# Gathering 48 of an encoder layer's tokens on all 128 partitions: 32 tokens in quarters and 16 in eighths, in place of 48 in halves on 96

## The chip, the cores and the metric

One core of a Trainium2 chip runs the whole layer. The metric is the device time of one execution in microseconds; the slowest (here the only) core counts.

## The reference, cut to what matters

One encoder layer on x of 512 tokens by 2048: a linear attention and a dilated window attention, then a mixer of 16,384 single-neuron experts. Only the mixer matters for the change:

```python
qry = (xt @ w_query).reshape(T, 8, 2, 128)
sc = jnp.einsum('thcd,hckd->thck', qry, sub_keys)          # 128 keys on either side, 8 heads
top_s, top_i = lax.top_k(sc, 16)                           # then the best 16 of the 256 pairs a head
idx   = expert numbers, 8 * 16 = 128 a token;  gates = softmax of their scores
u   = expert_down[idx]                                     # (tokens, 128, 2048)
act = gelu(einsum('tkd,td->tk', u, xn))
out = einsum('tk,tkd->td', gates * act, expert_up[idx])    # x = x + out
```

Every token has 128 slots, each with an expert's number and a gate. Both expert tables are 16,384 rows of 2048 float32, 8192 B a row.

## The kernel before

The layer goes through stages: the projections with both attentions (up to about 700 us of the profiled execution), the output projection, the queries with scores and top-k (about 900 to 1150 us), a stage that makes gate matrices (1200 to 1460 us), and the expert loop (1499 us to the end).

The 512 tokens are divided. **336 dense tokens** pass through all 16,384 experts on PE: `downT` (128 blocks `e` of 128 experts) gives the pre-activations, Gelu and the gates follow, and `upT` adds up the output. Each float32 product is made of three (`mm3`, lines 126 to 128), from a high part that ACT casts (line 77) and a low part that DVE subtracts (line 85; in the early blocks POOL does some). **128 tokens and 48 tokens** are gathered: for every slot an indirect DMA brings a row of an expert table per token, and DVE does the rest.

- The 128 tokens (`xn`, `idx[0]`, `gate[0]`, `ga[0]`) stand on 128 partitions, and a gather event handles one slot of each: 128 events a table.
- The 48 tokens (`xb`, `idx[1]`, ...) stand twice, on partitions 0 to 47 and 48 to 95. Lane h of a token handles half of its slots, so an event moves 96 rows and there are 64 of them. The two halves of the output are added on PE with the matrix `qs` at the end (line 1048).

`events` (line 1014) lists them: down rows of the 48, down rows of the 128, up rows of the 48 and one event that adds the tokens' x, up rows of the 128 and one such event; 386 in all. `gather(n)` (line 1036) fetches two events ahead, on POOL's queue, into one of three buffers `row`; for a down row DVE multiplies and sums (line 1042, into a column of `ga`), for an up row it adds the weighted row (line 1057). So an issue on POOL waits until DVE has read the buffer that it writes. `gather_next` is called 21 times in the gate stage, four times in the two blocks behind it, and then by `after()` (line 1273): spread evenly over the 448 steps of the loop but the last ten. A step is 24 matmuls: half of a `downT` block (`act_half`) or a granule of `upT`. After the last down event two steps go by before `weights_of_slots` makes the weights of the up rows.

The loop has 16 super-blocks of eight `e`. The first four have no `downT` steps: their 32 blocks were computed earlier and wait in DRAM (`pre_d`). Weights, `pre_d` and gates come on SP's queue.

**The gate stage.** For the dense tokens the gates become a matrix of 128 by 128 keys a token: one-hot rows `e` (DVE, line 1184, two buffers), times the gate (line 1187) and copied (ACT, line 1189), a matmul a token (line 1206), and a copy into `gs` (ACT, line 1208), which holds GT = 48 tokens. A full `gs` goes to DRAM `gt_d` on ACT's queue (line 1210). In the loop `fetch_gates` (line 1230) brings them back for four `e` at a time: 128 partitions, DENSE/GT groups, and in each a contiguous piece of 4 * GT numbers. The first two fetches are issued by POOL, in its queue between gathers.

The 48 tokens are prepared in three places: `turned_x` (line 776) transposes them with the others in the query stage, `gathered_slots` (line 1098) makes `idx` and `gate` and moves them to both halves by one matmul with the matrix `used` (line 1108), and POOL makes `used` and `qs` (lines 1009 and 1166).

Of the kernel before, what the change touches and what calls it, by code (L numbers as in the profile page):

```python
# [10 lines left out]
F32 = mybir.dt.float32  # L11
# [15 lines left out]
LB = 64  # L27
SPARE = 16
NB2 = LB - SPARE
PARTS = 128 // LB  # L30
GT = 48
LANES = (128, PARTS * NB2)
# [5 lines left out]
SLOTS = 128  # L38
LOW = -3.4e38
# [66 lines left out]
def layer(ctx, tc, A, out_t, out_g, out_b):  # L106
# [567 lines left out]
    rg = gn.tile([128, 2], F32, name="rg")  # L674
# [60 lines left out]
    xb = xnp.tile([LANES[1], D], F32, name="xb")  # L735
# [6 lines left out]
    sel_b = sp.tile([128, 3, SLOTS // PARTS], F32, name="sel_b")  # L742
# [19 lines left out]
    with ExitStack() as st:  # L762
# [13 lines left out]
        def turned_x(k, b):  # L776

            bank = pa()
            if b:
                t = tq.tile([128, 4, PARTS, NB2], F32, name="xr4")  # L780
                nc.scalar.copy(t, xq[:, 4 * k:4 * k + 4, SPARE:LB].unsqueeze(2).to_broadcast([128, 4, PARTS, NB2]))
            for c in range(4):
                src = t[:, c].rearrange("p a b -> p (a b)") if b else xq[:, 4 * k + c, LB:]
                nc.tensor.transpose(bank[:LANES[b], c * 128:(c + 1) * 128], src, ident)
            cs, n = slice(512 * k, 512 * k + 512), NB2 if b else 128
            xr = tq.tile([128, 512], F32, name="xr", bufs=2)
            nc.scalar.copy(xr[:n, :], bank[:n, :])
            nc.vector.tensor_tensor((xb if b else xn)[:, cs], bank[:LANES[b]], gains[k][:LANES[b]], op=OP.mult)
            nc.scalar.dma_start((x1b_d if b else x1g_d)[:, cs], xr[:n, :])
            if b and k + 2 < 4:  # L790
                gain_rows(k + 2)
# [4 lines left out]
        def rstd2():  # L796
            b = pa()
            for t in range(NB):
                nc.tensor.matmul(b[:, t:t + 1], sq[:, t * 128:(t + 1) * 128], ones[:, 0:1], start=True, stop=True)
            for h in range(PARTS):  # L800
                nc.tensor.matmul(b[LB * h:LB * h + LB, 4:5], sq[:, BASE:BASE + LB], ones[:, 0:1], start=True, stop=True)
            r = rsqrt(b[:, :5], 5, 1.0 / D)
            nc.vector.tensor_copy(rg, r[:, 3:5])
            return r
# [169 lines left out]
        for h in range(8):  # L974
            o = [pj() if h else pa() for _ in range(2)]
            for q in range(4):
# [19 lines left out]
                if 1 <= h < 5 and q % 2 == 0:  # L996
                    turned_x(h - 1, q // 2)
# [4 lines left out]
        n_slots = (SLOTS, SLOTS // PARTS)  # L1002
        idx = [slot.tile([128, n], I32, name=f"idx{b}") for b, n in enumerate(n_slots)]
        gate = [slot.tile([128, n], F32, name=f"gate{b}") for b, n in enumerate(n_slots)]
        ga = [slot.tile([128, n], F32, name=f"ga{b}") for b, n in enumerate(n_slots)]
        qs = slot.tile([128, NB2], F32, name="qs")
        lane = slot.tile([128, 2 * n_slots[1] + 1], F32, name="lane")
        used = slot.tile([128, PARTS, NB2], F32, name="used")
        nc.gpsimd.tensor_copy(used, ident.rearrange("p (a b) -> p a b", b=LB)[:, :, SPARE:])
        used = used.rearrange("p a b -> p (a b)")  # L1010
# [3 lines left out]
        events = [(up, b, k) for up in range(2) for b in (1, 0) for k in range(n_slots[b] + up)]  # L1014
        TURN = sum(n_slots)

        def fetch_rows(n):

            if n < len(events):
                up, b, k = events[n]  # L1020
                fetched[n] = t = rows.tile([128, D], F32, name="row", bufs=3)
                m = LANES[b]
                if k == n_slots[b]:
                    nc.gpsimd.dma_start(t[:NB2 if b else 128, :], (x1g_d, x1b_d)[b])
                else:
                    nc.gpsimd.indirect_dma_start(out=t[:m], out_offset=None, in_=A["up" if up else "down"],  # L1026
                                                 in_offset=bass.IndirectOffsetOnAxis(ap=idx[b][:m, k:k + 1], axis=0))

        def weights_of_slots():

            for b in range(2):
                g = ga[b][:LANES[b]]
                nc.scalar.activation(g, g, AF.Gelu_apprx_tanh, scale=rg[:LANES[b], b:b + 1])
                nc.vector.tensor_tensor(g, g, gate[b][:LANES[b]], op=OP.mult)

        def gather(n):
            fetch_rows(n + 2)
            up, b, k = events[n]
            m = LANES[b]
            t, x, g = fetched.pop(n)[:m], (xn, xb)[b][:m], ga[b][:m]  # L1040
            if not up:
                nc.vector.tensor_tensor_reduce(t, t, x, 1.0, 0.0, OP.mult, OP.add, g[:, k:k + 1])  # L1042
            elif k == n_slots[b]:
                if b:
                    for c in range(4):
                        cs = slice(c * 512, c * 512 + 512)
                        bank = pa()
                        nc.tensor.matmul(bank[:NB2, :], qs[:m], x[:, cs], start=True, stop=True)
                        nc.vector.tensor_tensor(t[:NB2, cs], t[:NB2, cs], bank[:NB2, :], op=OP.add)
                    nc.gpsimd.dma_start(out_b, t[:NB2, :])  # L1050
# [47 lines left out]
        def gathered_slots():  # L1098
# [4 lines left out]
            n, m = n_slots[1], LANES[1]  # L1103
# [3 lines left out]
            b = pa()  # L1107
            nc.tensor.matmul(b[:m, :2 * n + 1], used, lane, start=True, stop=True)
            nc.vector.tensor_copy(idx[1][:m], b[:m, 0:n])
            nc.scalar.copy(gate[1][:m], b[:m, n:2 * n])  # L1110
            nc.scalar.copy(rg[:m, 1:2], b[:m, 2 * n:2 * n + 1])
# [51 lines left out]
    with ExitStack() as st:  # L1163
        gp = pool(st, "gp")
        io4 = gp.tile([128, 128, 4], BF16, name="io4")
        nc.gpsimd.tensor_tensor(qs, ident[:, 0:NB2], ident[:, NB2:2 * NB2], op=OP.add)
# [11 lines left out]
        def one_hots(n):  # L1178
# [4 lines left out]
            e = gp.tile([128, 2, 128, 4], BF16, name="e", bufs=2)  # L1183
# [238 lines left out]
```

## Time and profile before

| | us |
|---|---|
| median of the three runs (lowest, highest) | 3423.83 (3418.21, 3429.88) |
| the profiled execution's own time | 3438.33 |
| its span, first to last instruction | 3436.6 |
| PE busy | 3196.3 (93%) |
| DVE busy | 2496.3 (73%) |
| ACT busy | 1163.0 (34%) |
| POOL busy | 1057.9 (31%) |
| DMA queue q1 (SP's loads), share of 16 engines' span | 33.3% |
| DMA queue q0 (POOL's gathers), share of 16 engines' span | 32.3% |
| moved by all queues | 811.09 MB |

The busy times are of engines that work side by side; they don't add up to the span. A share over the whole span mixes stages with different limits, so the stages are read apart. PE's matmuls are pipelined, and their records overlap.

### The profile page before, as it was taken

To read this page: it belongs to the slowest core of one execution; us is meant where nothing else is said; L and a number is where in the kernel's file an instruction comes from. 1 tells how busy PE (TensorE), PEld (TensorE's weight loads), DVE (VectorE), ACT (ScalarE), POOL (GpSimd) and SP (SyncE) were. 2 spreads that over 40 slices of the span, in tenths; PEclk is the share of its full clock that TensorE was granted. 3 is DMA by queue.
4 is the path that set the end of the run, shared out by engine and by line. 5 is a ranking of instruction groups with operands and counts; after the bars stand their busy time and mean duration, and the time that the engine had idled before them with its cause. 6 is when DMAs were issued, how large, how long until landed. Compare 5 with 4: busy or idle time off the path is not lost.

```text
span 3436.6 us, 47809 instructions
## 1 busy us (share of the span) xinstructions
PE 3196.3 (93%) x19012; PEld 2947.0 (86%) x19012; DVE 2496.3 (73%) x3830; ACT 1163.0 (34%) x1879; POOL 1057.9 (31%) x788
## 2 busy tenths in 40 slices
PE   8999999999999899967779999999889899999999
PEld 6777878788999899867679999899788799999999
DVE  5545353554468889957779888888777788989887
ACT  4334443443222355522223232232222222323322
POOL 3111010101245765512233333333332233333331
PEclk9999999999999999989899999999999999999999
DMA  4232222233322467699989999999899989999987
GB/s 144 86 97 78 86 74 86 86 131 139 101 94 78 133 225 256 227 283 259 249 280 352 352 354 358 358 363 339 242 266 271 266 315 350 365 347 382 354 344 269
DMA packets 151088, 811.09 MB, mean 236 GB/s; under 512 B 14736, under 2 KB 55024, under 8 KB 60912
## 3 DMA queue, kind: packets, MB, share of 16 engines
q1 hardware_dynamic: 86688, 390.69, 33.3%
q0 software_dynamic: 53888, 382.48, 32.3%
q10 hardware_dynamic: 10288, 34.87, 2.8%
q8 instruction: 149, 2.44, 0.3%
q14 instruction: 75, 0.61, 0.1%
HBM read 768.92 MB, written 39.06 MB: 235 GB/s over the span
## 4 chain that ended last, share of the span: by engine, by line
PE 39%; issue 24%; DVE 16%; DMA 10%; POOL 9%; ACT 2%; POOLq 0%; DVEq 0%; ACTq 0%
PE pj L128 10%; PE pj L126 10%; PE pj L127 10%; POOL row L1026 8%; DMA row<-in_up_dram,idx 5%; DMA wr4x<-in_upT_dram 3%; DVE e L1184 3%; DVE xn L1057 2%; DMA wr16x<-in_downT_dram 2%; DVE w L1187 2%; DVE row L1042 2%; DVE wl2x L85 1%; PE pa L609 1%; PE pa L550 1%; DVE wl8x L85 1%
## 5 line engine op out<-in xcount | busy, mean ns | idle before, releaser
L85 DVE TENSOR_TENSOR wl2x<-wr4x,wh2x 128x1024 fp32r<-128x1024 f32 x382 | 468.8, 1231 | 399.7 <-ACT wh2x L77 399.1
L128 PE MATMUL pj<-ah,wl2x 128*128 128x336 f32 x2048 | 673.7, 329 | 63.6 <-DVE wl2x L85 63.0
L126 PE MATMUL pj<-ah,wh2x 128*128 128x336 f32 x2048 | 665.1, 325 | 69.3 <-ACT wh2x L77 69.1
L127 PE MATMUL pj<-al,wh2x 128*128 128x336 f32 x2048 | 660.4, 322 | 2.4 <-DVE al L1259 2.4
L128 PE MATMUL pa<-yh,wl8x 128*128 128x336 f32 x1920 | 623.0, 324 | 40.9 <-DVE wl8x L85 38.8
L77 ACT CAST wh2x<-wr4x 128x1024 fp32r<-128x1024 f32 x382 | 394.6, 1047 | 750.6 <-DMA wr4x<-in_upT_dram 452.3
L126 PE MATMUL pa<-yh,wh8x 128*128 128x336 f32 x1920 | 622.3, 324 | 19.6 <-ACT wh8x L77 19.6
L127 PE MATMUL pa<-yl,wh8x 128*128 128x336 f32 x1920 | 613.4, 319 | 0.0
L1026 POOL DMA_INDIRECT row<-in_up_dram,idx x192 | 320.3, 1668 | 665.3 <-DVE xn L1057 381.9
L1026 POOL DMA_INDIRECT row<-in_down_dram,idx x192 | 308.4, 1606 | 629.0 <-DVE ga L1042 620.3
L128 PEld LDWEIGHTS pj<-ah,wl2x 128*128 128x128 f32 x2048 | 396.5, 194 | 92.8 <-DVE wl2x L85 90.9
L126 PEld LDWEIGHTS pj<-ah,wh2x 128*128 128x128 f32 x2048 | 397.9, 194 | 78.9 <-ACT wh2x L77 77.6
L128 PEld LDWEIGHTS pa<-yh,wl8x 128*128 128x128 f32 x1920 | 365.1, 190 | 63.3 <-DVE wl8x L85 56.1
L127 PEld LDWEIGHTS pj<-al,wh2x 128*128 128x128 f32 x2048 | 397.5, 194 | 4.4 <-DVE al L1259 3.3
L126 PEld LDWEIGHTS pa<-yh,wh8x 128*128 128x128 f32 x1920 | 366.9, 191 | 22.6 <-ACT wh8x L77 22.6
L127 PEld LDWEIGHTS pa<-yl,wh8x 128*128 128x128 f32 x1920 | 366.7, 191 | 0.0
L77 ACT CAST wh8x<-wr16x 128x1024 fp32r<-128x1024 f32 x256 | 265.3, 1046 | 248.0 <-DMA wr16x<-in_downT_dram 184.1
L85 DVE TENSOR_TENSOR wl8x<-wr16x,wh8x 128x1024 fp32r<-128x1024 f32 x200 | 249.1, 1246 | 99.9 <-ACT wh8x L77 99.7
L1042 DVE CUSTOM_DVE_ANT_0 row<-row,xn 128x2048 f32<-128x2048 f32 x128 | 292.5, 2285 | 26.7 <-DMA row<-in_down_dram,idx 26.7
L1057 DVE SCALAR_TENSOR_TENSOR xn<-row,ga,xn 128x2048 f32<-128x2048 f32 x127 | 297.9, 2346 | 10.2 <-DMA row<-in_up_dram,idx 10.2
L126 PE MATMUL pj<-wh2x,xh 128*128 128x512 f32 x704 | 284.8, 405 | 0.0
L127 PE MATMUL pj<-wl2x,xh 128*128 128x512 f32 x704 | 275.4, 391 | 1.3 <-DVE wl2x L85 1.3
(331 smaller groups left out, 5119.1 us busy)
## 6 DMA issues: line engine op xcount, KB each, us to landing
wr16x<-in_downT_dram SPq DMA_DIRECT2D x128, 1024.0 KB, 8.6
wr4x<-in_upT_dram SPq DMA_DIRECT2D x128, 1024.0 KB, 9.1
wr4x<-in_win_dram SPq DMA_DIRECT2D x47, 1024.0 KB, 4.9
gt_d<-gs ACTq DMA_DIRECT2D x7, 3072.0 KB, 12.4
g<-gt_d SPq DMA_DIRECT2D x30, 672.0 KB, 9.3
wr4x<-in_wout_dram SPq DMA_DIRECT2D x16, 1024.0 KB, 4.9
wr8x<-in_wq_dram SPq DMA_DIRECT2D x16, 1024.0 KB, 5.1
pre_d<-spill ACTq DMA_DIRECT2D x32, 168.0 KB, 4.4
```

What stands on the lines that cost most here:

```text
L77: self.nc.scalar.copy(hi, t)
L85: self.lo_engine[n].tensor_tensor(lo, t, hi.bitcast(F32), op=OP.subtract)
L126: nc.tensor.matmul(out, sh, mh, start=first, stop=False)
L127: nc.tensor.matmul(out, sh, ml, start=False, stop=False)
L128: nc.tensor.matmul(out, sl, mh, start=False, stop=last)
L550: nc.tensor.matmul(sc[u], qt[:, h, t * 128:(t + 1) * 128], kt[:, h, :], start=True, stop=True)
L609: nc.tensor.matmul(oo, vv[:, kb, h * 128:(h + 1) * 128], pt[u][:, kb, :], start=kb == 0, stop=kb == NB - 1)
L1026: nc.gpsimd.indirect_dma_start(out=t[:m], out_offset=None, in_=A["up" if up else "down"], in_offset=bass.IndirectOffsetOnAxis(ap=idx[b][:m ...
L1042: nc.vector.tensor_tensor_reduce(t, t, x, 1.0, 0.0, OP.mult, OP.add, g[:, k:k + 1])
L1057: nc.vector.scalar_tensor_tensor(x, t, g[:, k:k + 1], x, op0=OP.mult, op1=OP.add)
L1184: nc.vector.tensor_tensor(e, ij[:, :, ts].unsqueeze(2).to_broadcast([128, 2, 128, 4]), io4.unsqueeze(1).to_broadcast([128, 2, 128, 4]), op ...
L1187: nc.vector.tensor_tensor(w[:, 0], e[:, 0].rearrange("p k t -> p t k"), gd[:, ts].unsqueeze(2).to_broadcast([128, 4, 128]), op=OP.mult)
```

## The change

The 48 tokens are divided again, into 32 and 16. The 32 stand four times on the 128 partitions, each copy with a quarter of the slots (32 events a table); the 16 stand eight times, with an eighth each (16 events). With the 128 tokens that makes 176 events a table, all on 128 partitions; the rows that are moved stay the same. Each group has its own `x` (`xc` is new), `idx`, `gate`, `ga`, `qs`, and its own last event. To make room, GT becomes 28: twelve stores of a smaller `gs` for seven, and in `fetch_gates` twelve pieces of 448 B a partition for seven of 768 B. `e` gets a third buffer. The core of the diff:

```diff
-PARTS = 128 // LB
-GT = 48
-LANES = (128, PARTS * NB2)
+TOK = (NA, 32, 16)
+COL = (LB, SPARE, SPARE + 32)
+GT = 28
+N_SLOTS = tuple(SLOTS * n // 128 for n in TOK)
...
         def turned_x(k, b):
-            bank = pa()
+            bank, n, first = pa(), TOK[b], COL[b]
             if b:
-                t = tq.tile([128, 4, PARTS, NB2], F32, name="xr4")
-                nc.scalar.copy(t, xq[:, 4 * k:4 * k + 4, SPARE:LB].unsqueeze(2).to_broadcast([128, 4, PARTS, NB2]))
+                m = 128 // n
+                t = tq.tile([128, 4, 128], F32, name="xr4")
+                nc.scalar.copy(t.rearrange("p c (a b) -> p c a b", b=n), xq[:, 4 * k:4 * k + 4, first:first + n].unsqueeze(2).to_broadcast([128, 4, m, n]))
...
-                if 1 <= h < 5 and q % 2 == 0:
-                    turned_x(h - 1, q // 2)
+                if 1 <= h < 5 and q < 3:
+                    turned_x(h - 1, q)
...
+        for b in (1, 2):
+            n = TOK[b]
+            qs[b] = slot.tile([128, n], F32, name=f"qs{b}")
+            for a in range(128 // n):
+                if a == 0:
+                    nc.gpsimd.tensor_copy(qs[b], ident[:, 0:n])
+                else:
+                    nc.gpsimd.tensor_tensor(qs[b], qs[b], ident[:, n * a:n * a + n], op=OP.add)
+            used[b] = sp.tile([128, 2, n], F32, name=f"used{b}")
+            nc.gpsimd.tensor_copy(used[b], ident.rearrange("p (a b) -> p a b", b=LB)[:, :, COL[b]:COL[b] + n])
...
-        events = [(up, b, k) for up in range(2) for b in (1, 0) for k in range(n_slots[b] + up)]
-        TURN = sum(n_slots)
+        events = [(up, b, k) for up in range(2) for b in (2, 1, 0) for k in range(N_SLOTS[b] + up)]
+        TURN = sum(N_SLOTS)
...
-                    nc.gpsimd.indirect_dma_start(out=t[:m], out_offset=None, in_=A["up" if up else "down"],
-                                                 in_offset=bass.IndirectOffsetOnAxis(ap=idx[b][:m, k:k + 1], axis=0))
+                    nc.gpsimd.indirect_dma_start(out=t, out_offset=None, in_=A["up" if up else "down"],
+                                                 in_offset=bass.IndirectOffsetOnAxis(ap=idx[b][:, k:k + 1], axis=0))
...
-            b = pa()
-            nc.tensor.matmul(b[:m, :2 * n + 1], used, lane, start=True, stop=True)
+            bank = pa()
+            for b in (1, 2):
+                k, m, c = N_SLOTS[b], 2 * TOK[b], 128 * (b - 1)
+                u = used[b].rearrange("p a b -> p (a b)")
+                for a in range(n // k):
+                    to = slice(m * a, m * a + m)
+                    for q, src in enumerate((lane[:, k * a:k * a + k], lane[:, n + k * a:n + k * a + k])):
+                        nc.tensor.matmul(bank[to, c + k * q:c + k * q + k], u, src, start=True, stop=True)
+                    nc.tensor.matmul(bank[to, c + 2 * k:c + 2 * k + 1], u, lane[:, 2 * n:], start=True, stop=True)
...
-            e = gp.tile([128, 2, 128, 4], BF16, name="e", bufs=2)
+            e = gp.tile([128, 2, 128, 4], BF16, name="e", bufs=3)
```

How the list moves the gathers is seen on POOL, from the last gather of the gate stage on to the up rows of the 128 tokens (a number behind x counts rows that follow each other). Before:

```order
L1026 DMA row<-in_down_dram,idx_9887 96x2048
L1232 DMA g<-gt_d 128x7x192 x2
L1026 DMA row<-in_down_dram,idx_9887 96x2048 x41
L1026 DMA row<-in_down_dram,idx_9886 128x2048 x128
L1026 DMA row<-in_up_dram,idx_9887 96x2048 x64
L1024 DMA row<-x1b_d 48x2048
L1026 DMA row<-in_up_dram,idx_9886 128x2048 x2
L1050 DMA out_dram<-row 48x2048
L1026 DMA row<-in_up_dram,idx_9886 128x2048 x126
```

And now, where idx_9933 is that of the 16 tokens and idx_9932 that of the 32:

```order
L1034 DMA row<-in_down_dram,idx_9932 128x2048
L1245 DMA g<-gt_d 128x12x112 x2
L1034 DMA row<-in_down_dram,idx_9932 128x2048 x25
L1034 DMA row<-in_down_dram,idx_9931 128x2048 x128
L1034 DMA row<-in_up_dram,idx_9933 128x2048 x16
L1032 DMA row<-x1b_d 16x2048
L1034 DMA row<-in_up_dram,idx_9932 128x2048 x2
L1057 DMA out_dram<-row 16x2048
L1034 DMA row<-in_up_dram,idx_9932 128x2048 x30
L1032 DMA row<-x1b_d 32x2048
L1034 DMA row<-in_up_dram,idx_9931 128x2048 x2
```

Behind the two gate fetches 41 gathers of 96 rows became 25 of 128, and of the 64 up gathers on 96 partitions 48 on 128 were left; a second event of x and a second output stand between them.

On POOL at the end of the query stage, where `used` is made ahead of the first weight differences `wl8x` that PE waits for, before:

```order
L886 TENSOR_TENSOR sel_d<-oh 128x2x2x16
L1009 COPY used<-ident 128x96
L85 TENSOR_TENSOR wl8x_9954<-wr16x_9706,wh8x_9952 128x1024
L85 TENSOR_TENSOR wl8x_10009<-wr16x_9706,wh8x_10007 128x1024
L834 CAST tf<-ti 128x64
```

And now:

```order
L889 TENSOR_TENSOR sel_d<-oh 128x2x2x16
L1015 COPY qs_9941<-ident 128x32
L1017 TENSOR_TENSOR qs_9941<-qs_9941,ident 128x32 x3
L1019 COPY used_9946<-ident 128x64
L1015 COPY qs_9948<-ident 128x16
L1017 TENSOR_TENSOR qs_9948<-qs_9948,ident 128x16 x7
L1019 COPY used_9957<-ident 128x32
L86 TENSOR_TENSOR wl8x_10017<-wr16x_9751,wh8x_10015 128x1024
L86 TENSOR_TENSOR wl8x_10072<-wr16x_9751,wh8x_10070 128x1024
L837 CAST tf<-ti 128x64
```

One small copy became fourteen small operations; the sum `qs` of line 1166, which stood later, is among them.

## Rows read from the trace of the kernel before

**Rows 1.** The page of the profile: busy time of each engine with its share of the span, and three lines of the 40 equal slices of the span (85.9 us each): PE's and the DMA engines' busy tenths, and GB/s moved.

```profile
PE 3196.3 (93%) x19012; PEld 2947.0 (86%) x19012; DVE 2496.3 (73%) x3830; ACT 1163.0 (34%) x1879; POOL 1057.9 (31%) x788
...
PE   8999999999999899967779999999889899999999
...
DMA  4232222233322467699989999999899989999987
...
GB/s 144 86 97 78 86 74 86 86 131 139 101 94 78 133 225 256 227 283 259 249 280 352 352 354 358 358 363 339 242 266 271 266 315 350 365 347 382 354 344 269
```

**Rows 2.** Busy time by stage. Columns: the stage (us from the span's start), its length, then busy us and number of instructions of PE, PEld, DVE, ACT and POOL, the granted TensorE clock as a share, the mean busy share of the 16 DMA engines, and GB/s.

```profile
900.00:1030.00 130.00, 129.55 (x977) 126.68 (x976) 76.07 (x353) 37.40 (x77) 51.11 (x40) 1.00 0.28 92
1100.00:1200.00 100.00, 89.25 (x573) 86.35 (x573) 81.95 (x352) 32.69 (x79) 71.80 (x55) 0.93 0.38 123
1200.00:1460.00 260.00, 243.38 (x1711) 238.06 (x1710) 238.94 (x224) 132.34 (x206) 149.35 (x64) 0.99 0.71 234
1460.00:1499.20 39.20, 21.46 (x122) 20.48 (x120) 14.35 (x16) 8.04 (x11) 6.42 (x6) 0.76 1.01 323
1499.20:1766.00 266.80, 208.64 (x1176) 194.89 (x1176) 190.50 (x236) 72.67 (x108) 64.32 (x39) 0.89 0.92 257
1836.20:2389.00 552.80, 525.53 (x3306) 510.98 (x3305) 483.65 (x535) 169.87 (x208) 181.11 (x113) 0.99 0.94 358
2413.00:2752.00 339.00, 293.63 (x1735) 279.81 (x1734) 262.03 (x226) 89.97 (x110) 101.84 (x61) 0.94 0.97 262
2793.00:3372.00 579.00, 551.68 (x3457) 534.89 (x3456) 514.73 (x447) 179.06 (x221) 196.86 (x119) 0.99 0.93 356
3372.00:3433.00 61.00, 59.52 (x384) 58.43 (x382) 40.67 (x43) 16.58 (x18) 5.79 (x5) 1.00 0.69 250
```

**Rows 3.** DMA queues in the stage 2413 to 2752 us (up rows of the 48 tokens): packets, MB, share of 16 engines' time. q0 carries what GpSimd issues (the gathers), q1 what SP issues (weights, gates).

```profile
q0 software_dynamic: 6759, 47.52, 56.2%
q1 hardware_dynamic: 9741, 41.18, 40.0%
```

**Rows 4.** The same for 2793 to 3372 us (up rows of the 128 tokens).

```profile
q0 software_dynamic: 17080, 124.33, 53.8%
q1 hardware_dynamic: 17664, 81.01, 38.5%
```

**Rows 5.** The same for 1499 to 1766 us (down rows of the 48 tokens).

```profile
q0 software_dynamic: 4558, 32.10, 46.8%
q1 hardware_dynamic: 13757, 36.25, 44.9%
```

**Rows 6.** Who waited for whom from 1836 to 3372 us: us in total, times, longest.

```profile
ACT wh2x L77 <- DMA wr4x<-in_upT_dram: 315.3, 64, 13.3
...
ACT wh8x L77 <- DMA wr16x<-in_downT_dram: 175.2, 46, 10.5
...
POOL row L1026 <- DVE ga L1042: 376.7, 115, 7.5
```

**Rows 7.** Groups of instructions by line and form, of the whole span: count, then busy us, mean ns of one, and the idle time ahead of them with what ended it.

```profile
L1042 DVE CUSTOM_DVE_ANT_0 row<-row,xn 128x2048 f32<-128x2048 f32 x128 | 292.5, 2285 | 26.7 <-DMA row<-in_down_dram,idx 26.7
...
L1057 DVE SCALAR_TENSOR_TENSOR xn<-row,ga,xn 128x2048 f32<-128x2048 f32 x127 | 297.9, 2346 | 10.2 <-DMA row<-in_up_dram,idx 10.2
...
L1026 POOL DMA_INDIRECT row<-in_down_dram,idx x192 | 308.4, 1606 | 629.0 <-DVE ga L1042 620.3 <-DVE al L1259 3.6 <-issue 3.1
```

**Rows 8.** DMA queue q10 (what ACT issues) from 206 to 246 us, where it stores the linear attention's turned output in pieces of 512 B: packets, MB, share of 16 engines' time.

```profile
q10 hardware_dynamic: 2109, 1.05, 8.9%
```

**Rows 9.** Instructions in order of time at the end of the one-hot stage (ACT's, then POOL's, then DVE's): start, us, engine, line, operation, and in brackets the idle time ahead of it and what ended it.

```profile
1464.77 0.33 ACTq L1210 DMA_DIRECT2D gt_d<-gs  x1
...
1479.88 1.04 ACT L77 CAST wh8x<-wr16x 128x1024 fp32r<-128x1024 f32 x1 [13.61 <-DMA pre<-pre_d]
...
1477.82 1.98 POOL L1232 DMA_DIRECT2D g<-gt_d  x2 [18.80 <-issue]
...
1494.64 2.29 DVE L1042 CUSTOM_DVE_ANT_0 row<-row,xb 96x2048 f32<-96x2048 f32 x1 [12.46 <-DMA row<-in_down_dram,idx]
```

**Rows 10.** The stores of the gates (L1210): time from issue to landing, least, median and most, of the seven.

```profile
DMA to landing us min/median/max: 10.4/12.4/13.7
```

**Rows 11.** The one-hot tiles' groups, by line and form (columns as in rows 7).

```profile
L1184 DVE TENSOR_TENSOR e<-ij,io 128x1024 bf16<-128x1024 bf16 x84 | 125.5, 1494 | 3.4 <-ACT ij L117 3.4
...
L1189 ACT CAST w<-e 128x512 f32<-128x512 bf16 x84 | 56.1, 669 | 115.1 <-DVE e L1184 113.9 <-DVE w L1187 1.2
```

**Rows 12.** Groups by line and form from 900 to 1200 us (columns as in rows 7): the transposes of the gathered tokens, the index matmul, and two set-up operations of POOL.

```profile
L784 PE MATMUL pa<-ident,xr 128*96 128x128 f32 x16 | 2.4, 272 | 0.0
...
L1108 PE MATMUL pa<-lane,used 128*96 128x129 f32 x2 | 0.4, 290 | 0.0
...
L1009 POOL COPY used<-ident 128x96 f32<-128x96 f32 x1 | 0.3, 263 | 0.0
...
L1166 POOL TENSOR_TENSOR qs<-ident 128x48 f32<-128x48 f32 x1 | 0.7, 733 | 0.0
```

**Rows 13.** The reduction of the 48 tokens at the end of the up rows, lines 1048 and 1049: count, ns of one (least, median, most), first and last start, and form.

```profile
L1048 PE MATMUL pa<-xb,qs x8: 592/592/630, 2766.3 to 2769.4; 96*48 96x512 f32 x8
L1049 DVE TENSOR_TENSOR row<-row,pa x4: 678/678/678, 2767.4 to 2770.0; 48x512 f32<-48x512 f32 x4
```

More of the change, by code (lines that the diff above doesn't have):

```diff
@@ L734, in layer @@
     xn = xnp.tile([128, D], F32, name="xn")
-    xb = xnp.tile([LANES[1], D], F32, name="xb")
+    xb = xnp.tile([128, D], F32, name="xb")
+    xc = xnp.tile([128, D], F32, name="xc")
     slot2 = work.enter_context(ExitStack())
@@ L799, in rstd2 @@
                 nc.tensor.matmul(b[:, t:t + 1], sq[:, t * 128:(t + 1) * 128], ones[:, 0:1], start=True, stop=True)
-            for h in range(PARTS):
+            for h in range(2):
                 nc.tensor.matmul(b[LB * h:LB * h + LB, 4:5], sq[:, BASE:BASE + LB], ones[:, 0:1], start=True, stop=True)
             r = rsqrt(b[:, :5], 5, 1.0 / D)
-            nc.vector.tensor_copy(rg, r[:, 3:5])
+            nc.vector.tensor_copy(rg[:, 0:2], r[:, 3:5])
             return r
@@ L1001, in layer @@
         slot = pool(ctx, "slot", side="right")
[L1002 to L1010, printed above, removed]
+        idx = [slot.tile([128, n], I32, name=f"idx{b}") for b, n in enumerate(N_SLOTS)]
+        gate = [slot.tile([128, n], F32, name=f"gate{b}") for b, n in enumerate(N_SLOTS)]
+        ga = [slot.tile([128, n], F32, name=f"ga{b}") for b, n in enumerate(N_SLOTS)]
+        lane = sp.tile([128, SLOTS + 1], F32, name="lane")
+        qs, used = {}, {}
+        for b in (1, 2):
[8 more added lines that the diff above has]
+            nc.gpsimd.tensor_copy(used[b], ident.rearrange("p (a b) -> p a b", b=LB)[:, :, COL[b]:COL[b] + n])
         spill = pool(ctx, "spill", side="right")
@@ L1021, in fetch_rows @@
                 fetched[n] = t = rows.tile([128, D], F32, name="row", bufs=3)
[L1022 to L1027 removed]
+                if k == N_SLOTS[b]:
+                    nc.gpsimd.dma_start(t[:TOK[b], :], (x1g_d, x1b_d[0:32], x1b_d[32:48])[b])
+                else:
+                    nc.gpsimd.indirect_dma_start(out=t, out_offset=None, in_=A["up" if up else "down"],
+                                                 in_offset=bass.IndirectOffsetOnAxis(ap=idx[b][:, k:k + 1], axis=0))
         def weights_of_slots():
[L1031 to L1034, printed above, removed]
+            for b in range(3):
+                g = ga[b]
+                nc.scalar.activation(g, g, AF.Gelu_apprx_tanh, scale=rg[:, b:b + 1])
+                nc.vector.tensor_tensor(g, g, gate[b], op=OP.mult)
         def gather(n):
```

36 lines of the change are left out of this document (17 added, 19 removed).

## The prediction

> **What bounds the kernel now.** I read the 40 slices first, then stages cut out of them, then the DMA queues of those stages. PE is busy 93% of the span, but not evenly: there are dips at 1400 to 1800 us and at 2400 to 2800 us, and in both the DMA engines are at 9 tenths while they move only some 250 GB/s; where PE is at 9, they move about 355 [rows 1]. The dips lie in the expert loop, which begins at 1499 us. I count it in steps: one pass of the weights' half or granule, 24 matmuls on PE (eight tiles by three products, or four tiles by two experts by three). So 1176 matmuls in 266.8 us are 49 steps of 5.45 us, 1735 in 339 us are 72.3 steps of 4.69, and the two stages between and behind take 3306/24 = 137.8 steps of 4.01 and 144 steps of 4.02. The last 16 steps, ten of which have no gather, take 3.81 [rows 2]. The two slow stages are those in which the 48 tokens are gathered on 96 partitions (first the down rows, then the up rows); in the others 128 tokens are gathered on 128.
>
> The DMA share does not tell them apart (0.92 and 0.97 against 0.94 and 0.93, same rows); the price of a row does. In the slow up stage the gathers' queue moved 47.52 MB, 5801 rows of 8192 B, in 56.2% of 16 engines' 339 us: 525 ns a row [rows 3]. In the quick up stage it is 53.8% of 16 x 579 us for 15,177 rows: 328 ns [rows 4]. In the slow down stage 1999 us for 3918 rows: 510 ns [rows 5]. The weights' queue suffers with it, 52.7 against 44.0 us per MB [rows 3, 4]. What ends last there is the DMA: the casts on ACT wait 315 and 175 us for weight transfers, while the gathers' issues wait for DVE, that is for a free buffer, and not the reverse [rows 6]. So DMA engines bound the slow stages; the quick stages lie close to three limits at once (DMA 0.93, PE 551.68 of 579, DVE 514.73).
>
> **The change, part by part.** I sum against the profiled execution's 3438.3 us; the median of the runs shown is 14.5 us below that.
>
> *Gathers.* Each pass has 176 events instead of 192 for the same 22,528 rows, and all are on 128 partitions. I take 328 ns a row for all: only the partition count differs between the two up stages. The ends are 328 (as quick) and 525 (no change). [...]
>
> Per step: before, 361 events (386 less 25 ahead of the loop) over 438 steps are 0.824, 79 rows a step with the 48 tokens and 105.5 with the 128; now 330 over 438 are 0.753, 96.4 rows everywhere.
>
> - First 49 steps. Need now 0.92 x 5.45 = 5.0 us of DMA a step. After: gathers 96.4 x 328/16 = 1.98 instead of 2.55; the other queue 2.45 [rows 2, 5] x 44.0/52.7 = 2.04; 0.11 of the rest and small pieces; together 4.13, at the same share 4.49 a step. Gain 47 us (58 at a share of 0.97). The next 15 steps gain 3.
> - The 282 quick steps need 0.93 x 4.02 = 3.74 a step; nine rows fewer take 0.19 off, small pieces add 0.04: 3.59. The last 16 steps need 0.69 x 3.81 = 2.63 and take 3.81. A straight line between the two gives 3.99 at 3.59; the lower end is 3.81. I take the middle, 3.90, since waits should grow quicker than the load. Gain 32 us (7 to 58).
> - The 72.3 slow up steps become such steps: 4.69 to 3.90, gain 57 us (51 to 64).
>
> DVE loses 32 products of some 2.3 us and POOL 32 issues of 1.6 [rows 7]. I count nothing for either: DVE's are covered by PE and DMA, and POOL waits for DVE [rows 6]. If DVE were the limit, its share is the rival below.
>
> *Small pieces of the gates.* GT = 28 instead of 48 makes a fetch of 672 KB 1536 pieces of 448 B instead of 896 of 768 B. No row has 448 B. Pieces of 512 B took 8.9% of 16 x 40 us over 2048, 28 ns at most [rows 8]; one of 768 B is then between 28 and 42. A fetch costs 0.3 to 1.1 us of DMA time more; I take 0.6, about 19 us over 32 fetches, which stands in the needs above. The other end is a doubled piece, 56 ns.
>
> *Stores of the gates, third buffer of e.* Twelve stores of 1.8 MB replace seven of 3.1. The last one stands on the path into the loop: issued at 1464.77, landed when POOL's gate fetch goes at 1477.8 after 18.8 us idle, and ACT's next store and cast wait as long [rows 9, 10]. 28/48 of 12.4 us saves 5 (0 to 8: the two fetches behind it, which hold up DVE's row for 12.5 us, get longer). The third buffer saves nothing: DVE waits 3.4 us in all before e, and ACT's 114 us before its half are for DVE, which is 92% busy there [rows 2, 11].
>
> *Ahead of the gathers.* 16 more transposes at 0.15 us and their copies stand where PE is full (129.55 of 130): 2.4 us on the path; DVE and ACT are at 76 and 37 of 130 there and cover theirs. 18 small matmuls of two records replace one, 34 records more at 0.15 to 0.29: 5 to 10 us of PE at a place that is 89% busy, between waits; I count 4. POOL gets 14 small operations for one ahead of the weight differences that PE waits for (and one fewer later): 13 at 0.26 to 0.73 is 3.4 to 9.5; half of that is hidden in POOL's 28% idle: 3. Together 9 (3 to 15) [rows 2, 12].
>
> *Last event of each group.* There are two reductions instead of one: four matmuls of two records and four DVE additions, about 3.4 us in a full loop; 4 [rows 13].
>
> Sum: -47 -3 -32 -57 +9 -5 +4 = -131 us, so 3307 for the profiled execution, 3293 at the median's level. The lower ends together give -175, **3249**; the upper ones -90, 3334.
>
> **Rivals.**
> 1. *Full relief*: the quick steps fall to 3.81, PE's own pace, as in the tail. -175: 3249. For it: PE is then the only full engine. Against: DVE stays near 0.86, in order, and the tail had hardly a gather.
> 2. *DVE or the chain of casts holds 4.01 a step.* For it: DVE is at 0.89 in the quick stages. Then the quick steps gain nothing, the slow up steps 49: -88, 3336.
> 3. *Short pieces cost double.* 1536 x 56 against what was taken is 2.8 us more a fetch: 0.175 a step lifts the need to 3.76, so the steps stay at 4.02 (the up stage of the 48 gains 48, the other 282 steps 0), and the first 64 steps, with a fetch every eight, lose 0.38 each, 24 of their 50. -66: 3358. For it: no row shows a fetch below 512 B. Against: 512, and the straight proportion to larger ones, show no step. [...]
> 4. *The price does not come from the partitions but from the 48 tokens' rows* (slower). The rows stay at 515 ns, now 128 at a time: a step of these stages needs 3.10 + 1.88 + 0.07 (the other queue as it is [rows 3]), 5.2 us at the same share, for 64 steps instead of 78, while 170 others take 3.92 instead of 155 at 4.02: 10 us more a pass. With the 8 us of the fixed parts that is +28: 3452. It decides from the price: 12,288 rows make 7.7 us per 10 ns, so above some 480 ns there is no gain left. Against: the down and the up tables both show it, with the same tokens' indices but other data, and the weights' transfers in the same stages slow too, though they read nothing of those rows.
>
> **How the numbers follow.** The forecast (3293, own range 3260 to 3325) gets 0.60, rival 1 0.15, rival 2 0.10, rival 3 0.10, rival 4 0.05. Forecast, 1, 2 and 3 are faster by more than 0.3% (10 us, about what a measurement here can tell); I move 0.02 of them to no change for a mixture of 2 and 3. Low is 3240, below rival 1; high is 3360, just above rival 3, which leaves out rival 4 and some tails.
>
> **What would show it.** Right: the price of a row on the gathers' queue is near 328 ns from the first stage of the loop to the last, at some 350 GB/s; there is no dip of PE at 2400 to 2800; the steps of the up pass take 3.9 us. Rival 1 shows as 3.8, rival 2 as 4.0 with DVE above 0.9 and DMA below 0.9, rival 3 as 4.0 with the weights' queue share grown by more than 3 points at the same MB, rival 4 as a price of 500 in the first third of each pass. The front is right if the loop begins at 1499 + 4 us (-5 to +15). The prediction is wrong if the slow stages' rows get cheaper and the steps there still take over 4.4 us.

## The result, and the profile after

The changed kernel takes **3280.7 us** (median of four runs, 3272.0 to 3285.0) against 3424.8 for the kernel before beside it: a ratio of 0.958, 95% interval 0.955 to 0.960. That is 12 us below the forecast and inside its own range, with two errors behind it that happen to cancel in part.

The profiled execution took 3272.0 us, the lowest of its four; that of before lay 14.5 us above its median. So the profiles differ by 166 us and the medians by 144, and the terms below, which come from profiles, add up to 166.

From the page after: the engines, PE, DMA and GB/s in 40 equal slices (81.8 us each), and the stores of the gates (KB each, median us to landing).

```profile
PE 3145.6 (96%) x19070; PEld 2922.8 (89%) x19070; DVE 2435.3 (74%) x3792; ACT 1168.0 (36%) x1890; POOL 1006.7 (31%) x770
...
PE   8999999999999989987899999999999999999999
...
DMA  4222222224322247779889999999989999999996
GB/s 152 78 88 96 75 94 71 91 97 146 125 90 79 80 145 264 265 270 340 322 335 339 358 362 358 360 350 352 348 334 364 349 343 358 358 364 358 358 358 251
...
gt_d<-gs ACTq DMA_DIRECT2D x12, 1792.0 KB, 6.7
```

Against [rows 1] the second dip of PE is gone and the first is shallower (8, 7, 8 in the 18th to 20th slice): from the 21st slice on PE stands at 9, and from the 19th on GB/s is never below 320 until the tail. By stage (columns as in [rows 2]):

```profile
900.00:1030.00 130.00, 121.27 (x895) 117.39 (x894) 68.29 (x305) 36.16 (x71) 43.44 (x33) 0.99 0.26 86
1473.20:1508.70 35.50, 25.07 (x157) 24.23 (x155) 18.94 (x19) 10.90 (x16) 10.59 (x8) 0.93 0.90 327
1508.70:1799.20 290.50, 259.49 (x1537) 247.51 (x1538) 237.15 (x288) 91.06 (x126) 78.47 (x48) 0.94 0.89 335
1799.20:2352.00 552.80, 543.00 (x3479) 533.29 (x3479) 487.65 (x542) 180.32 (x225) 177.88 (x109) 1.00 0.93 355
2410.00:2590.00 180.00, 179.94 (x1140) 174.00 (x1138) 159.95 (x150) 58.71 (x74) 57.62 (x37) 1.00 0.93 351
2660.00:3206.00 546.00, 538.18 (x3457) 530.50 (x3457) 489.36 (x433) 178.72 (x220) 187.47 (x108) 1.00 0.94 358
```

At 24 matmuls a step: 1537 are 64 steps of 4.54 us; 3479 are 145 steps of 3.81; 1140 (nearly all up rows of the 32 tokens) 47.5 steps of 3.79; 3457 are 144 steps of 3.79. The up stage that took 4.69 a step now goes at the pace of the others. The one row that got worse is the first: PE, which was full in 900 to 1030 us [rows 2], issues 82 matmuls fewer there.

The queues of three stages: 1508.7 to 1742 us (down rows of the 48 until 1649, then of the 128), 2410 to 2590 and 2660 to 3206 (columns as in [rows 3]).

```profile
q1 hardware_dynamic: 18440, 37.44, 46.8%
q0 software_dynamic: 5378, 39.09, 40.8%
...
q0 software_dynamic: 4954, 35.87, 50.8%
q1 hardware_dynamic: 8101, 27.14, 41.6%
...
q0 software_dynamic: 15636, 113.81, 52.3%
q1 hardware_dynamic: 22768, 80.97, 41.7%
```

The price of a row, share x 16 x stage / (MB / 8192 B): 319, 334 and 329 ns, where it was 510, 525 and 328 [rows 3 to 5]. The weights' queue costs 45.0 us a MB in the last stage (44.0 in [rows 4]) with all its short pieces.

### The profile page after: what moved, and what is told of

It reads as the page before. It is cut to its first block, busy times and chain, and to the rows that moved or that the text cites. A ratio compares the mean times of both kernels' runs of the same rounds, so it can differ in the third digit from the quotient of the medians.

```text
span 3270.2 us, 47842 instructions
## 1 busy us (share of the span) xinstructions
PE 3145.6 (96%) x19070; PEld 2922.8 (89%) x19070; DVE 2435.3 (74%) x3792; ACT 1168.0 (36%) x1890; POOL 1006.7 (31%) x770
## 4 chain that ended last, share of the span: by engine, by line
PE 46%; DVE 22%; issue 17%; DMA 7%; POOL 5%; ACT 3%; DVEq 0%; POOLq 0%; SPq 0%; ACTq 0%
PE pj L129 12%; PE pj L127 12%; PE pj L128 12%; POOL row L1034 5%; DVE row L1049 3%; DVE e L1197 3%; DMA wr4x<-in_upT_dram 3%; DVE xn L1064 3%; DVE wl8x L86 2%; DMA wr16x<-in_downT_dram 2%; DVE wl2x L86 2%; DVE w L1200 2%; PE pa L129 2%; PE pa L127 2%; PE pa L128 2%
## 5 line engine op out<-in xcount | busy, mean ns | idle before, releaser
L129 PE MATMUL pj<-ah,wl2x 128*128 128x336 f32 x2048 | 661.6, 323 | 26.8 <-DVE wl2x L86 26.5
L127 PE MATMUL pj<-ah,wh2x 128*128 128x336 f32 x2048 | 655.1, 320 | 27.2 <-ACT wh2x L78 26.9
L128 PE MATMUL pj<-al,wh2x 128*128 128x336 f32 x2048 | 652.3, 319 | 2.5 <-DVE al L1272 2.5
L78 ACT CAST wh2x<-wr4x 128x1024 fp32r<-128x1024 f32 x382 | 394.8, 1048 | 656.2 <-DMA wr4x<-in_upT_dram 373.1
L129 PE MATMUL pa<-yh,wl8x 128*128 128x336 f32 x1920 | 610.7, 318 | 5.6 <-DVE wl8x L86 4.6
L1034 POOL DMA_INDIRECT row<-in_up_dram,idx x176 | 300.5, 1707 | 587.8 <-DVE xn L1064 389.0
L1034 POOL DMA_INDIRECT row<-in_down_dram,idx x176 | 278.8, 1584 | 572.0 <-DVE ga L1049 557.9
L129 PEld LDWEIGHTS pj<-ah,wl2x 128*128 128x128 f32 x2048 | 389.5, 190 | 47.4 <-DVE wl2x L86 46.4
L127 PEld LDWEIGHTS pj<-ah,wh2x 128*128 128x128 f32 x2048 | 390.2, 191 | 33.7 <-ACT wh2x L78 32.3
L128 PEld LDWEIGHTS pj<-al,wh2x 128*128 128x128 f32 x2048 | 390.1, 190 | 4.1 <-DVE al L1272 3.2
L86 DVE TENSOR_TENSOR wl8x<-wr16x,wh8x 128x1024 fp32r<-128x1024 f32 x200 | 247.4, 1240 | 72.3 <-ACT wh8x L78 72.2
```

The lines of the kernel that those rows point to most:

```text
L78: self.nc.scalar.copy(hi, t)
L86: self.lo_engine[n].tensor_tensor(lo, t, hi.bitcast(F32), op=OP.subtract)
L127: nc.tensor.matmul(out, sh, mh, start=first, stop=False)
L128: nc.tensor.matmul(out, sh, ml, start=False, stop=False)
L129: nc.tensor.matmul(out, sl, mh, start=False, stop=last)
L1034: nc.gpsimd.indirect_dma_start(out=t, out_offset=None, in_=A["up" if up else "down"], in_offset=bass.IndirectOffsetOnAxis(ap=idx[b][:, k:k ...
```

## The experiments

**The same kernel again**, for the size of differences that mean nothing.

> The changed kernel once more, beside the three runs that follow on the same chip. 3272 to 3285 us; the profile again shows rows at 309 to 319 ns on the gathers' queue through the whole loop, the loop's first tile near 1509 us and the last 384 steps at 3.82 us. If one of these moves by more than its share of the time's spread, differences of that size in the runs beside it mean nothing.

Measured: 3278.3 us, 0.957 (0.955 to 0.960); the loop's first tile at 1507.4 us; a gathered row's packet takes 331 ns on the average of the whole run (309 in the median), against 330 (309) in the changed kernel. Over the same 144 steps of the last stage the trace gives 3.78 us a step, against 3.79 in the changed kernel; in all five profiles of kernels that do the same work there (the changed one twice, and the variants below with the calls spread, with early copies, and with two DMAs of 64) it lies between 3.78 and 3.85, and in the four that do what the kernel before does (that one, with small granules, and with 112 and 128 partitions), between 4.01 and 4.03. The 138 steps of the 128 tokens' down rows vary more: 3.79 to 3.86 in seven kernels that run them as the changed one does, and 3.91 to 4.01 in six that run them as the kernel before does, whose own profile is the slowest of the six.

**Is it the partitions or the rows?** The kernel before, with 32 useless rows more in each event of the 48 tokens, so that it fills 128 partitions:

```diff
+MOVED = (128, 128)
...
-                m = LANES[b]
+                m = MOVED[b]
...
```

DVE still works on 96; the lines that give the further 32 rows their indices are left out.

> The kernel before with one thing changed: the gathers of the 48 tokens move 128 rows instead of 96, the 32 further ones fetched with indices of the same tokens into partitions that nothing reads. So 49,152 rows instead of 45,056, and DVE works on 96 partitions as before. Theory (the price belongs to the 96 partitions): 310 to 330 ns a row from the first stage to the last, the slow stages gone (3.9 to 4.0 us a step), about 3340 us, although 9% more rows move. Rival 4 of the prediction (the price belongs to these tokens' rows): 500 ns or more in these stages with a third more rows, steps above 5.2 us, 3500 us or more.

Measured: 3345.7 us, 0.976 (0.972 to 0.979): 79 us gained although it moves 9% more rows. The stages of the up rows (of the 48, then of the 128), and q0 in the first of them:

```profile
2360.00:2665.00 305.00, 287.37 (x1798) 277.09 (x1797) 269.03 (x233) 91.90 (x112) 119.13 (x63) 0.99 0.93 350
2695.00:3275.00 580.00, 551.94 (x3458) 536.44 (x3458) 514.98 (x447) 179.56 (x222) 195.77 (x118) 0.99 0.93 355
...
q0 software_dynamic: 8848, 64.36, 54.0%
```

335 ns a row, and 4.07 us a step with the same tokens' indices and the same tables. Rival 4 is out. The last 144 steps, untouched, stay at 4.03. The changed kernel is 65 us faster still; by this subtraction, which no run isolates, that is what its fewer events are worth together with its dearer front and small granules.

**How many partitions are enough?** 112 in the kernel before (`MOVED = (128, 112)`), and in the changed kernel two DMAs of 64 instead of one of 128:

```diff
-                    nc.gpsimd.indirect_dma_start(out=t, out_offset=None, in_=A["up" if up else "down"],
-                                                 in_offset=bass.IndirectOffsetOnAxis(ap=idx[b][:, k:k + 1], axis=0))
+                    for m in (slice(0, 64), slice(64, 128)) if b else (slice(0, 128),):
+                        nc.gpsimd.indirect_dma_start(out=t[m], out_offset=None, in_=A["up" if up else "down"],
+                                                     in_offset=bass.IndirectOffsetOnAxis(ap=idx[b][:m.stop - m.start, k:k + 1], axis=0))
```

> The kernel before with the gathers of the 48 tokens on 112 partitions (16 rows more an event that nothing reads; DVE on 96 as before). Between 96 (510 to 525 ns a row) and 128 (328): if the price follows the fullest of 16 equal shares of the partitions, 8 against 7 on the average, it is 8/7 of 328, 375 ns, and the slow stages take 4.0 to 4.2 us a step; if any count that doesn't split evenly pays alike, 470 ns or more and 4.6 us or more.

> The changed kernel with each gather of the 32 and the 16 tokens issued as two DMAs of 64 partitions each, 0 to 63 and 64 to 127 (the second takes the indices of the first, so its output is not the reference's). Number of rows, of events and all other work as in the changed kernel, 144 more issues on POOL. [...]

Measured, one run each: 3453.6 us and 3455.9 us, beside 3417.3 for the kernel before. The stage of the 48 tokens' up rows with 112 partitions, and q0 in it:

```profile
2420.00:2779.00 359.00, 307.66 (x1799) 293.32 (x1798) 269.60 (x233) 91.99 (x112) 93.00 (x63) 0.94 0.97 275
...
q0 software_dynamic: 7872, 56.36, 58.8%
```

With two times 64:

```profile
2397.00:2758.00 361.00, 275.85 (x1525) 257.07 (x1523) 220.14 (x197) 79.02 (x96) 122.08 (x95) 0.88 0.96 238
...
q0 software_dynamic: 7475, 48.91, 58.4%
```

With 112 that is 491 ns a row and 4.79 us a step, with two times 64 it is 565 ns and 5.68 us. For 112 that is the second of its two expectations. So a price in proportion to the fullest share is out (375 expected for 112), and a count that divides the 128 evenly, as 64 does, is not cheap for that reason: of 64, 96, 112 and 128 partitions only 128 is cheap, and 112 is nearly as bad as 96. Issuing two halves back to back doesn't mend it. Why a row costs more on fewer partitions no run here shows. What the runs show is the step between 112 and 128, and that weights' packets of the same stages slow with the rows (52.1 us a MB with 112 and 59.1 with 64, from q1's shares, against 44.0).

**The small granules alone**: GT = 28 and three buffers of `e` in the kernel before.

> The kernel before with only the smaller gate granules (GT 28, so 448-byte pieces and 1.8 MB stores) and the third buffer of e; gathers as before. Theory: the granules' worth is the shorter last store ahead of the loop, 5 to 8 us, and small pieces cost next to nothing: 3412 to 3425 us, with the slow stages still at 4.7 and 5.4 us a step. Rival 3 of the prediction (short pieces cost double): 448-byte pieces at 50 ns or more, and 3450 to 3520 us. Other rival: the transition has no share, 3424 us and the loop's first tile at 1499.

Measured: 3431.9 us over 12 runs, 1.003 (1.000 to 1.005). Both stages of the up rows stay as they were, 4.69 and 4.02 us a step:

```profile
2413.00:2752.00 339.00, 293.49 (x1734) 280.95 (x1733) 260.21 (x224) 88.65 (x107) 92.48 (x60) 0.94 0.98 263
2790.00:3357.00 567.00, 541.05 (x3384) 525.35 (x3383) 501.78 (x436) 176.39 (x218) 190.95 (x116) 0.98 0.93 355
```

The theory's sign was wrong: the granules cost some 7 us (1 to 16) rather than saving any. The loop does begin earlier, though by 3.4 us only (1495.8 us instead of 1499.2). The weights' queue costs 45.1 us a MB in the last stage instead of 44.0, which is 0.04 us of DMA need a step, as the prediction had it; but the steps of both up stages stay as they were, so where the 7 us arise the traces don't show. Rival 3 is out all the same: the packets of 448 B take 25 ns in the median in the changed kernel's trace and those of 768 B took 36 in that of before, so a short piece costs little more than its share by size (21) and far from the doubled 56.

**The front.** PE's waits from 900 to 1110 us in the changed kernel (us in total, times, longest); before had none for this line:

```profile
PE pa L787 <- ACT xr L784: 10.1, 8, 1.7
```

Instructions at the first of them (start, us, engine, line; in brackets the idle time ahead):

```profile
931.66 0.62 ACT L784 COPY xr<-xq 128x512 f32<-128x512 f32 x1
932.33 0.66 PE L787 MATMUL pa<-ident,xr 128*128 128x128 f32 x4 [0.97 <-ACT xr L784]
...
933.02 0.58 ACT L790 COPY xr<-pa 32x512 f32<-32x512 f32 x1 [0.74 <-PE pa L787]
...
933.63 0.69 DVE L791 TENSOR_TENSOR xb<-pa,g2b 128x512 f32<-128x512 f32 x1 [3.65 <-ACT xr L790]
```

The copy that spreads the tokens is issued right ahead of the transposes that need it, behind two score copies on ACT; PE stands idle for it, 0.97 us here, and DVE 3.65 us ahead of its product, with the top-k pieces behind that (the next begins at 934.24 us). Two edits move the calls without changing their work:

```diff
-                if 1 <= h < 5 and q < 3:
-                    turned_x(h - 1, q)
+                if 1 <= h < 7 and q % 2 == 0:
+                    turned_x(*divmod(2 * (h - 1) + q // 2, 3))
```

> The changed kernel with its twelve turned_x calls spread out: two a head over six heads (at q = 0 and q = 2) instead of three a head over four heads; the work is the same. Theory: the front's loss is the place of the third call, not its count of work: PE waits for the copy xr4 on ACT (1.3 to 1.9 us before each of its transposes at q = 1) and DVE's product stands late ahead of the top-k pieces. Then those waits shrink to the level of the calls at q = 0, the query stage ends near 1121 us instead of 1134, and the kernel takes 10 to 13 us less than the changed kernel beside it, about 3269. Rival: the front pays for the work itself (16 transposes, 8 copies, 4 products) wherever it stands: then no change within 3 us, and the stage ends near 1134 again.

and, on top of it, the copy of call i + 1 made at the end of call i (`copy_x(i + 1)` behind the copy `xr`):

> The changed kernel with the twelve turned_x calls spread over six heads, and the copy xr4 of a call made at the call before it, so that PE need not wait for it. Theory: PE's gaps of over 0.4 us in the four heads with calls (13.3 us in the changed kernel, 6.2 with the spreading alone, 0.6 in the kernel before) fall to some 1 us; the loop begins at 1495 to 1500 us instead of 1508, and the kernel takes 8 to 13 us less than the changed kernel, 3265 to 3270. Rival: the remaining gaps come from ACT's order and not from the copy: then 1501 as with spreading alone.

PE's waits in the same window, with the calls spread:

```profile
PE pa L787 <- ACT xr L784: 4.1, 4, 1.1
```

and with the copies early as well, where this line is gone and the longest-lasting one is

```profile
PE pa L949 <- DVE qT L945: 0.8, 4, 0.2
```

| | changed | spread | spread, early copy | before |
|---|---|---|---|---|
| last query matmul, us | 1135.0 | 1125.9 | 1121.6 | 1119.0 |
| loop begins, us | 1508.7 | 1500.8 | 1496.7 | 1499.2 |
| time, us | 3280.7, 3278.3 | 3273.9 | 3267.7 | 3424.8 |

Spreading ended the query stage 9 us earlier (13 were expected) and took 4 to 7 us off the time (10 to 13 were expected); the early copy ended the stage another 4 us earlier: 13 of the query stage's 16 us were the place of the work, and 2.6 the work, for which the prediction had 2.4. The times follow (ratios 0.956, 0.953 to 0.958, and 0.954, 0.952 to 0.956), but each interval overlaps that of the changed kernel; the places in the trace are the firmer evidence.

**What holds the quick steps?** Two runs of the changed kernel, in the stage of the last 128 up events: half the rows not fetched, and half of DVE's addition left out.

```diff
+                if up and b == 0 and k % 2 == 1 and k < N_SLOTS[b]:
+                    fetched[n] = fetched_last[0]
+                    return
...
+                fetched_last[0] = t
```

```diff
-                nc.vector.scalar_tensor_tensor(x, t, g[:, k:k + 1], x, op0=OP.mult, op1=OP.add)
+                w = slice(0, D if b else D // 2)
+                nc.vector.scalar_tensor_tensor(x[:, w], t[:, w], g[:, k:k + 1], x[:, w], op0=OP.mult, op1=OP.add)
```

> The changed kernel with half of the up rows of the 128 tokens left out: every second event uses the row fetched for the one before it, so DVE, ACT, POOL's other work and PE do what they did, and the DMA moves 48 rows a step less in the stage after some 2660 us (its output is not the reference's). In that stage the changed kernel takes 3.78 to 3.80 us a step; PE's own pace there is 3.65 to 3.71. If the DMA engines set what is left above PE's pace, the steps fall to 3.70 or less; if DVE or the casts set it, they stay at 3.78 or above.

> The changed kernel with half of DVE's work on the same events left out: each up row of the 128 tokens is added over half of its columns only (its output is not the reference's); all rows are fetched. The other half of the pair: if DVE sets what is left above PE's pace, the steps after 2660 us fall to 3.70 or less and DMA's share rises above 0.95; if the DMA does, they stay at 3.78 or above.

Half the rows:

```profile
2690.00:3200.00 510.00, 506.74 (x3274) 502.36 (x3273) 462.82 (x411) 169.32 (x210) 97.55 (x51) 1.00 0.72 258
```

Half of DVE's addition:

```profile
2690.00:3190.00 500.00, 500.00 (x3258) 500.00 (x3257) 364.27 (x411) 170.98 (x208) 123.59 (x103) 1.00 0.94 369
```

3.74 us a step with DMA at 0.72, and 3.68 with PE busy without a gap. So **PE's own pace in these steps is 3.68**, and the changed kernel stands 0.11 above it. Taking away a quarter of the DMA's load gives back 0.05 of that, taking away half of DVE's additions all of it: DVE's additions hold these steps more than the DMA does, the DMA has a part in it, and the two overlap. Half the rows gave neither of the outcomes expected of it (3.70 or less, 3.78 or more). Each is one execution.

The same in the kernel before, at the size by which the change moves each: one row in twelve not fetched, or 1872 of 2048 columns added.

> The kernel before with one in twelve up rows of the 128 tokens not fetched (the event uses the row before it; the output is not the reference's): 8% fewer rows a step, as the change brings to this stage, and DVE's work as before. In the stage behind some 2790 us the kernel before takes 4.02 us a step and the changed one 3.79. If the rows a step (the DMA) set the quick steps, as the prediction's line from 4.02 to 3.81 assumed, they come to 3.80 to 3.90; if DVE does, they stay at 3.97 to 4.05.

> The kernel before with DVE's up additions of the 128 tokens over 1872 of 2048 columns (the output is not the reference's): 8.6% less of this work a step, as the change's fewer events bring, and all rows fetched. If DVE's events set the quick steps (the prediction counted nothing for DVE's 32 products), they come from 4.02 to 3.80 to 3.90 behind 2790 us; if the DMA does, they stay at 3.97 to 4.05. If both this run and the one before give some 3.9, the two limits are shared about evenly.

For each of the two, first the 138 steps of the 128 tokens' down rows, which the edits don't touch, then the 144 steps that [rows 2] has from 2793 to 3372 us. With fewer rows:

```profile
1836.00:2376.00 540.00, 521.74 (x3314) 507.40 (x3313) 483.43 (x537) 169.57 (x208) 181.04 (x114) 1.00 0.95 366
2782.30:3359.20 576.90, 554.69 (x3456) 540.14 (x3457) 515.75 (x447) 178.94 (x221) 185.02 (x109) 0.98 0.89 339
```

that is 4.01 us a step in the second, and with less DVE work 3.97:

```profile
1836.00:2381.60 545.60, 522.76 (x3312) 508.83 (x3311) 483.86 (x537) 169.30 (x208) 182.03 (x114) 1.00 0.94 363
2772.70:3343.90 571.20, 546.09 (x3456) 536.41 (x3457) 494.54 (x447) 179.69 (x221) 194.76 (x119) 0.99 0.93 361
```

Of the 0.23 us that the change gives these steps, fewer rows alone give 0.01, inside the spread of 4.01 to 4.03, and less DVE time alone 0.05. Both are single executions, and the untouched down steps differ from those of before by more (3.91 and 3.95 against 4.01), so these two runs say only that neither load alone makes the 0.23. Whom PE waited for there (us, times, longest), first in the kernel before, 2793 to 3372 us,

```profile
PE pa L128 <- DVE wl8x L85: 12.3, 19, 1.3
PE pj L126 <- ACT wh2x L77: 6.7, 2, 4.0
PE pj L128 <- DVE wl2x L85: 6.7, 12, 1.4
PE pa L126 <- ACT wh8x L77: 1.1, 1, 1.1
```

then in the changed kernel, 2660 to 3206 us:

```profile
PE pj L129 <- DVE wl2x L86: 6.4, 8, 1.1
PE pa L129 <- DVE wl8x L86: 1.1, 3, 0.6
```

The waits for ACT's casts went (7.8 us), and those for DVE's low parts fell from 19.0 us to 7.5. The change takes 8.6% of the **events** away, and with them rows, DVE time and the order in which both are asked for: a step without an event, in which DVE could catch up, came every 5.7 steps before (0.824 events a step) and comes every 4 now (0.753). Whether it is this rhythm that makes the whole worth more than its parts wasn't tried and stays open.

**One instruction off DVE**, on top of the spread calls and early copies: the product of the pre-activations and gates goes to POOL.

```diff
-                nc.vector.tensor_tensor(v, v, gates[self.e // 4][:, :, self.e % 4, :], op=OP.mult)
+                nc.gpsimd.tensor_tensor(v, v, gates[self.e // 4][:, :, self.e % 4, :], op=OP.mult)
```

> The kernel of the run before this with the product of pre and the gates moved from DVE to POOL (some 0.5 us for every fourth loop step on DVE). Theory: with 128 partitions everywhere DVE's order is what keeps steps above PE's own 3.65 to 3.71, so 0.13 us of DVE a step less gives back some 0.03 to 0.1 us of the 0.11 a step: 10 to 35 us, 3235 to 3258 us. Rival: POOL takes longer for it and stands behind its gather issues, which wait for DVE, so the weight differences come late: no gain, or 10 to 40 us slower.

Measured: **3248.1 us**, 0.948 (0.945 to 0.950), 20 us below the run beside it (0.954, 0.952 to 0.956) and the best of all, though the instruction itself is dearer:

```profile
L1276 POOL TENSOR_TENSOR pre<-pre,g 128x336 f32<-128x336 f32 x128 | 233.1, 1824 | 175.6 <-ACT pre L1273 137.7 <-issue 36.7 <-DMA g<-gt_d 1.0
```

1.82 us on POOL for 0.50 on DVE. The profiles show some 6.5 us at the loop's start (1490.2 us instead of 1496.7): in the changed kernel the first product stands behind a gather event that waits for its row,

```profile
1504.13 2.29 DVE L1049 CUSTOM_DVE_ANT_0 row<-row,xb 128x2048 f32<-128x2048 f32 x1 [7.27 <-DMA row<-in_down_dram,idx]
1506.34 0.08 DVE L1049 DVE_READ_ACCUMULATOR2_ANT ga<- 128x1 f32 x1
1506.34 0.50 DVE L1266 TENSOR_TENSOR pre<-pre,g 128x336 f32<-128x336 f32 x1
```

and on POOL it doesn't. In the loop the profiles show little. A stretch of the down rows, then the same 144 steps of the last stage, without this edit and with it:

```profile
1800.00:2350.00 550.00, 539.61 (x3442) 528.92 (x3441) 484.21 (x537) 180.32 (x225) 173.55 (x108) 1.00 0.93 354
2653.30:3197.60 544.30, 537.94 (x3458) 530.55 (x3458) 490.10 (x435) 178.63 (x220) 182.10 (x109) 1.00 0.94 360
...
1800.00:2350.00 550.00, 544.15 (x3495) 535.77 (x3494) 492.71 (x504) 181.76 (x226) 258.51 (x149) 1.00 0.94 360
2642.50:3190.40 547.90, 538.18 (x3459) 530.60 (x3457) 491.28 (x395) 180.14 (x222) 271.56 (x147) 1.00 0.94 356
```

The down steps get quicker (3.84 to 3.78 us), the last ones don't (3.78 and 3.80), and the whole loop is shorter by 2.1 us. The two profiles differ by 8.7 us, the medians by 20 (one profile is the fastest of its five runs, the other the slowest), so where the rest comes from isn't shown, nor that DVE's order is what the move relieved.

## Why the prediction was right, and where it wasn't

| term of the sum, us | predicted | profiles |
|---|---|---|
| first 64 steps | -50 | -46 (337.0 to 290.5) |
| slow up steps, 72.3 | -57 | -64 (4.69 to 3.80) |
| quick steps, 282 | -32 | -61 (4.01 to 3.81 and 4.02 to 3.79) |
| last events, transitions between stages | +4 | -4 |
| up to the one-hots, and these | +9 | +18 |
| gate store and loop's start | -5 | -8 |
| sum | -131 | -166 |

- **The price of a row**: right. 328 ns was taken for all, 319 to 334 came, and the padded kernel, at 335, shows that the partitions make it. What makes a row dear on fewer of them stays open: the estimate by the fullest of 16 equal shares gave 375 for 112 partitions, and 491 were measured.
- **First 64 steps, slow up steps**: right within 4 and 7 us. The 7 are the next point's miss: these steps, too, were to take 3.90. That the DMA ends last there was read from waits of 1836 to 3372 us [rows 6], most of them of the quick stages; in the slow up stage alone the casts wait 78.0 and 49.7 us of 339 for weights, and the padded kernel bears the reading out.
- **Quick steps**: the mechanism was mistaken and the term half its size. The prediction drew a line over the DMA's need, from 4.02 to the tail's 3.81, called 3.81 PE's own pace, and counted nothing for DVE's 32 products since PE and the DMA would cover them. All three failed: fewer rows alone move next to nothing (4.01), PE's own pace is 3.68, and in before's last stage PE waited 19.0 us for DVE and 7.8 for ACT's casts. The pace that came, 3.80, is that of rival 1; its cause isn't (PE isn't the only full engine, DVE still delays it). What makes the 0.2 us a step stays open. Some 10 of the 61 us belong to one execution rather than to the change: the profile of before takes 4.01 a step in the down rows, five kernels like it there 3.91 to 3.99.
- **Front**: mis-sized twice, in opposite directions. The added transposes cost 16 us instead of 2.4, 13 of them by their place, since ACT and DVE, counted as covered at 37 and 76 of 130 us, deliver late (PE waits 10.1 us for `xr`). The small matmuls and POOL's operations, put at 7, cost about 1: the query stage ends 16.0 us later and the first one-hot comes 17.1 later, and the 36 records of these matmuls begin between 1186.8 and 1188.4 us.
- **Gate store**: -8 instead of -5, at the end of its range. The store lands in 6.7 us instead of 12.4 [rows 10]. The granules alone bring the loop only 3.4 us forward in the kernel before, so the rest of the 8 has another cause, which wasn't looked for; as a whole they don't pay by themselves.
- **The level**: the prediction put the new kernel 14.5 us below its profile, as before; its profile turned out 8.7 below its median. That hid 23 us of the 35 by which the sum was short, so it is luck that the forecast came within 12 us.
- **The range's lower end**: -175 takes the lower ends of the gathers' terms only; with those of the front and of the store it is -184, or 3240.
- **The other rivals**: 2 would have shown steps of 4.0, 3 dearer short pieces, 4 dear rows in the first third of each pass; none did.

## What to carry to other kernels

Price a gather by the row in each stage before changing anything: two stages with nearly the same busy share of the DMA engines differed by a factor of 1.6 in what a row cost, and filling the partitions with useless rows was already worth 79 us. A share of busy time says that an engine is full, not which cut will help: halving one load at a time told that DVE's additions held the last steps more than the DMA did, though that was at 0.94. Compare the same steps, and look at a stage that the edit doesn't touch: it tells how far one profile differs from the next. And where work is added on an engine that is full (PE, 129.55 of 130 us), ask when its operand is made: issued one call earlier, the same copy kept PE waiting no more (4.1 us with the calls spread).

## What the runs showed of the hardware

- Rows of 8192 B gathered onto 64 (twice), 96, 112 and 128 partitions cost 565, 525, 491 and 335 ns each of DMA engine time: a step at 128, not a slope. The weights' packets of the same stages pay with them: 59.1, 52.7, 52.1 and 44.6 us a MB.
- The granted clock of TensorE ahead of the loop was 0.76 on the average of 39.2 us in which PE was busy for 21.5 [rows 2], a mean of stretches at 1.00 (1460 to 1475 us) and at 0.50 (1480 to 1485 us among them); it is 0.93 in the 35.5 us that now lead to the loop, with PE busy for 25.1. Over the loop's first 64 steps 0.90 became 0.94.
- The same product of 128 x 336 numbers took 0.50 us on DVE and 1.82 us on POOL on the average, and moving it still paid.
